# Two heads' attention scores in one product, with decay and mask as a tile from GpSimd

## The chip, the core and the metric

The kernel runs on one core of a Trainium2 chip. A core has a tensor engine (TensorE, PE in the profile), a vector engine (VectorE, DVE), a scalar engine (ScalarE, ACT), GpSimd (POOL), and a sync engine (SyncE, SP), which here only issues DMAs. They run side by side, each through its own queue in order, and wait for each other by semaphores. SBUF is the on-chip memory; products land in PSUM, from which VectorE and ScalarE read. The metric is the device time of one execution in microseconds.

## The reference

One streaming step of a small encoder: 256 new frames of one stream (the prompt) and 64 new frames of another, which has 256 past frames in a cache (the sample). There are two layers; each is a SwiGLU channel mixer, a token mixer and a second channel mixer. The first layer's token mixer is a gated convolution, the second's is the forgetting attention, which the change touches:

```python
def fox_attend(q, k, v, c_q, c_k, q_pos, k_pos):
    s = jnp.einsum('bqhd,bkhd->bhqk', q, k) * (HEAD_DIM ** -0.5)
    decay = c_q[..., :, None] - c_k[..., None, :]        # per head; sums of log forget gates
    mask = k_pos[None, :] <= q_pos[:, None]
    s = jnp.where(mask, s + decay, NEG_INF)
    p = jax.nn.softmax(s, axis=-1)
    return jnp.einsum('bhqk,bkhd->bqhd', p, v)
```

There are 16 heads of 64 channels. The prompt's 256 queries see the prompt's keys at or before them; the sample's 64 queries see the 256 cached keys and the sample's own keys at or before them.

## The kernel before

All 320 frames (256 of the prompt, 64 of the sample) go through the dense products together, features on the partitions and frames along the free axis. Each weight comes from memory in slabs of 1024 x 256 (`wr`), is split by ScalarE into a rounded part (`wh`, line 121) and by VectorE into the rest (`wl`, line 122), and each dense product is three products of 320 columns (lines 141 to 143). Three slabs fit in each pool, so a new slab is loaded and split when an old one has been multiplied.

The attention layer works on pairs of heads, eight in all; a pair fills 128 partitions. The projections give q, k and v of a pair (`pq`, `pk`, `pv`), and four generators follow them:

- `gates` makes the log forget gates and their running sums, negated and scaled for the keys (`nck`) and scaled for the queries (`cq`), one row per head.
- `decay_rows` loads these rows into the operands of the score product.
- `qk_heads` turns q and k frame-major (`qt`), normalises them (`sq` on GpSimd, then VectorE), turns them back (`np`), and writes them, with the cached keys (`kps`), to `qa` and `ka`. For each head these have its 64 channels in one half of the partitions; in the other half are zeros but for two rows, one of ones and one with the decay. So one product over 128 rows gives scores plus decay.
- `attend` makes the scores. The sample queries of both heads come first, as two products of 64 columns of queries each (`ss`, line 625), then each head's prompt queries in two blocks of 128 over 128 and 256 keys (`sc`, line 632), the second head's some dense products later. Each block goes through `softmax`: line 612 adds the mask and takes the row's extreme, line 614 exponentiates and sums, lines 615 and 616 divide. Then the probabilities are transposed (`tps`, `tpp`), copied by ScalarE (`pst`, `ppt`) and multiplied by the values into `oT` (lines 663 to 671). The sample's own values lie on 64 rows of the third tile of `vtok`.

Four PSUM banks (`aux`) serve all of these small products; a fifth request waits until the oldest bank is read out.

The order on TensorE is written out by a small planner at the end of `attn_mixer`. It walks through the dense products at 0.41 a group of three and puts in each step of a generator as soon as its delay (`LAT`, and the numbers that the generators yield) is over. The other engines' order is made by a scheduler from the program's order and the buffers. GpSimd's and SP's queues hold what they issue in that order, whatever is ready.

Of the kernel before, what the change touches and what calls it, by code (L numbers as in the profile page):

```python
# [16 lines left out]
P = 128  # L17
D = 1024
KD = D // P
S = 256  # L20
# [25 lines left out]
def trunk_kernel(  # L46
# [21 lines left out]

    def aux(name):
# [75 lines left out]
    # ---------------------------------------------------------------- constants and inputs  # L145
# [11 lines left out]
    # the first products' operands come in pieces of a few contraction tiles  # L157
# [26 lines left out]
    # ---------------------------------------------------------------- residual stream and norms  # L184
# [51 lines left out]
    # ---------------------------------------------------------------- x in  # L236
# [62 lines left out]
    # ---------------------------------------------------------------- attention: constants and small inputs  # L299
# [5 lines left out]
    for g, src in ((gq, q_norm), (gk, k_norm)):  # L305
        for hh in range(2):
# [4 lines left out]
    mask1 = const.tile([P, 2 * P], F32, tag="mask1", name="mask1")  # L311
    nc.gpsimd.memset(mask1, 0.0)
    nc.gpsimd.affine_select(out=mask1[:, P:], in_=mask1[:, P:], compare_op=ALU.is_ge, fill=NEG,
                            base=0, pattern=[[-1, P]], channel_multiplier=1)
    masks = const.tile([P, PAST + TS], F32, tag="masks", name="masks")
    nc.gpsimd.memset(masks, 0.0)
    for hh in range(2):
        m = masks[hh * TS:(hh + 1) * TS, 0:TS]
        nc.gpsimd.affine_select(out=m, in_=m, compare_op=ALU.is_ge, fill=NEG, base=0,
                                pattern=[[-1, TS]], channel_multiplier=1)  # L320

    # Per pair of heads: rows of one head's channels, and in the other half two rows that add
    # the decay c_q - c_k to the scores.
    qa, ka = [], []
    for b in range(2):
        q = const.tile([P, 2, T], F32, tag=f"qa{b}", name=f"qa{b}")
        k = const.tile([P, 2, NK], F32, tag=f"ka{b}", name=f"ka{b}")
        for t in (q, k):
            nc.gpsimd.memset(t[0:HD, 1], 0.0)
            nc.gpsimd.memset(t[HD:P, 0], 0.0)  # L330
            nc.gpsimd.memset(t[HD:HD + 2, 0], 1.0)
            nc.gpsimd.memset(t[0:2, 1], 1.0)
        qa.append(q)
        ka.append(k)
    # ones where a frame counts into the sum of a later one
# [10 lines left out]
    # ---------------------------------------------------------------- channel mixer  # L346
# [76 lines left out]
    # ---------------------------------------------------------------- gated convolution  # L423
# [54 lines left out]
    # ---------------------------------------------------------------- forgetting attention  # L478
    def attn_mixer(next_gain, pool):
# [3 lines left out]
        cq = pool.tile([H, T], F32, tag="cq", name="cq")  # L483
        r2T = pool.tile([P, 3], F32, tag="r2T", name="r2T")
        st = {"decay": False, "rows": set(), "scored": [0] * KD, "v": set(), "done": [0] * KD}

        def gates(pf):
            fr = pool.tile([H, T], F32, tag="fr", name="fr")
# [7 lines left out]
            # forget gates, frame-major  # L496
# [13 lines left out]
            # log1p(e) = 2 artanh(e / (2 + e))  # L510
# [14 lines left out]
            # sums of the log gates up to each frame, head-major: prompt; past and sample  # L525
# [10 lines left out]
            TSC(cq[:, 0:S], cp[:H, 0:S], 8.0, None, ALU.mult)  # L536
            TSC(cq[:, S:T], cs[:H, PAST:PAST + TS], 8.0, None, ALU.mult)
            st["decay"] = True
            yield 1.8, 0.0

        def decay_rows(p):
            while not (st["decay"] and (p < 2 or st["scored"][p - 2] == 2)):
                yield 0.0, 0.0
            b = p % 2
            for hh in range(2):
                h = 2 * p + hh
                row = HD if hh == 0 else 0
                nc.sync.dma_start(out=ka[b][row:row + 1, hh], in_=nck[h:h + 1])
                nc.sync.dma_start(out=qa[b][row + 1:row + 2, hh], in_=cq[h:h + 1])
            yield 0.0, 4.0  # L550
            st["rows"].add(p)

        def qk_heads(p, pq, pk, kpast, vpast, vtok):
# [5 lines left out]
            # normalised per head, frame-major; the gains are left for later  # L559
# [22 lines left out]
            ktok = pool.tile([P, 3, P], F32, tag="ktok", name="ktok", bufs=2)  # L582
# [12 lines left out]
            nc.scalar.copy(out=ka[b][0:HD, 0, T:NK], in_=kps[0:HD, 0:PAST])  # L595
            nc.vector.tensor_copy(ka[b][HD:P, 1, T:NK], kps[HD:P, 0:PAST])
            for n, g, dst in zip(qkn, (gq, gk), (qa[b], ka[b])):
# [3 lines left out]
                nc.scalar.activation(dst[0:HD, 0, 0:T], np_[0:HD, :T], AF.Copy, scale=g[0:HD])  # L601
                TSC(dst[HD:P, 1, 0:T], np_[HD:P, :T], g[HD:P], None, ALU.mult)
# [228 lines left out]
```

## Time and profile before

| what | value |
|---|---|
| median of the runs | 1251.88 us (1251.42 to 1253.5, 3 runs) |
| the profiled execution, first to last instruction | 1250.0 us |
| TensorE, VectorE, ScalarE, GpSimd busy | 1238.3, 763.0, 499.4, 52.2 us |
| attention stage (from the first q projection to the last output projection) | 832 to 1009 us |

The profiled execution shows one time, its span; the runs' median is 1.9 us above it. In the timeline a row is a start, a duration, the engine, the line, the operation, what it writes and reads, and the shape; `x4` is four records in a row, and a float32 product is two records, a transpose or one of the rounded dense products one. Durations of products overlap, so that the distance between starts tells what a product takes from the stream. A bracket at a row's end is the engine's idle time before it and what ended it. A row of waits has the total, the number and the longest. A row of a tile has the least, median and greatest duration in ns. A row of stretches has length, busy time of PE, PEld, DVE, ACT and POOL, granted clock, DMA share and GB/s.

### The profile page before, as it was taken

Reading aid. Unit: us, or ns where it says so; the run is one execution under the profiler, and the core shown is the slowest. Engines: PE = TensorE matmul, PEld = TensorE weight load, DVE = VectorE, ACT = ScalarE, POOL = GpSimd, SP = SyncE. Lnnn points to the kernel's source line nnn. Section 1 sums busy time; section 2 is a strip of 40 time slices with the busy share of each in tenths; the row PEclk is TensorE's granted clock in tenths of the full one; section 3 lists DMA queues with packets and bytes.
Section 4 is the critical chain, followed back from the end, with each engine's and each line's share of the span. In section 5 each row is a group of like instructions: output and inputs, shape, how many; then the busy total and the mean of one; then the engine's idle time right before and its main releaser. Section 6 shows DMA issues by size and latency. Waiting matters only on the chain.

```text
span 1250.0 us, 20886 instructions
## 1 busy us (share of the span) xinstructions
PE 1238.3 (99%) x8520; PEld 1216.8 (97%) x8520; DVE 763.0 (61%) x1403; ACT 499.4 (40%) x797; POOL 52.2 (4%) x102
## 2 busy tenths in 40 slices
PE   9999999999999999999999999999999999999998
PEld 7999999999999999999999999998898899999998
DVE  5756645576685656554665564558887676666432
ACT  6434333333433434333343433334656544343321
POOL 5000000000000000000000000002222000000000
PEclk9999999999999999999999999999999999999999
DMA  8544444444445444344444444454333154443440
GB/s 258 192 159 145 148 140 152 155 150 146 158 136 161 143 153 151 126 155 159 153 151 144 160 128 151 126 172 120 111 126 122 51 192 146 146 158 129 162 136 22
DMA packets 186128, 180.93 MB, mean 145 GB/s; under 512 B 8644, under 2 KB 185952, under 8 KB 186032
## 3 DMA queue, kind: packets, MB, share of 16 engines
q1 hardware_dynamic: 184880, 178.95, 44.4%
q8 instruction: 67, 1.10, 0.4%
q10 hardware_dynamic: 768, 0.54, 0.2%
q0 software_dynamic: 384, 0.11, 0.2%
q14 instruction: 29, 0.24, 0.1%
HBM read 175.54 MB, written 3.97 MB: 144 GB/s over the span
## 4 chain that ended last, share of the span: by engine, by line
PE 93%; DVE 4%; issue 1%; DMA 1%; ACT 1%; POOL 1%; POOLq 0%; ACTq 0%; SPq 0%; DVEq 0%
PE po L142 8%; PE po L143 8%; PE po L141 8%; PE pa L141 8%; PE pa L142 8%; PE pb L143 8%; PE pb L142 8%; PE pa L143 8%; PE pb L141 8%; PE pc L142 2%; PE pc L141 2%; PE pc L143 2%; PE pm L142 2%; PE pm L143 2%; PE pm L141 1%; DVE wl L122 1%
## 5 line engine op out<-in xcount | busy, mean ns | idle before, releaser
L122 DVE TENSOR_TENSOR wl<-wr,wh 128x1024 fp32r<-128x1024 f32 (+2 forms) x340 | 399.2, 1196 | 174.9 <-ACT wh L121 171.1
L121 ACT CAST wh<-wr 128x1024 fp32r<-128x1024 f32 (+2 forms) x337 | 333.5, 1018 | 423.6 <-issue 190.4
L141 PE MATMUL po<-gh,wh 128*128 128x320 f32 x704 | 217.0, 308 | 0.0
L142 PE MATMUL po<-gl,wh 128*128 128x320 f32 x704 | 216.5, 308 | 0.0
L143 PE MATMUL po<-gh,wl 128*128 128x320 f32 x704 | 216.5, 308 | 0.0
L141 PE MATMUL pa<-xh,wh 128*128 128x320 f32 x688 | 213.0, 310 | 0.0
L143 PE MATMUL pa<-xh,wl 128*128 128x320 f32 x688 | 213.0, 310 | 0.0
L142 PE MATMUL pa<-xl,wh 128*128 128x320 f32 x688 | 212.9, 310 | 0.0
L141 PE MATMUL pb<-xh,wh 128*128 128x320 f32 x688 | 212.8, 309 | 0.0
L142 PE MATMUL pb<-xl,wh 128*128 128x320 f32 x688 | 212.8, 309 | 0.0
L143 PE MATMUL pb<-xh,wl 128*128 128x320 f32 x688 | 212.8, 309 | 0.0
L142 PEld LDWEIGHTS po<-gl,wh 128*128 128x128 f32 x704 | 131.9, 187 | 0.0
L141 PEld LDWEIGHTS po<-gh,wh 128*128 128x128 f32 x704 | 131.9, 187 | 0.0
L143 PEld LDWEIGHTS po<-gh,wl 128*128 128x128 f32 x704 | 131.9, 187 | 0.0
L141 PEld LDWEIGHTS pa<-xh,wh 128*128 128x128 f32 x688 | 129.3, 188 | 0.1
L143 PEld LDWEIGHTS pa<-xh,wl 128*128 128x128 f32 x688 | 129.3, 188 | 0.0
L142 PEld LDWEIGHTS pa<-xl,wh 128*128 128x128 f32 x688 | 129.3, 188 | 0.0
L141 PEld LDWEIGHTS pb<-xh,wh 128*128 128x128 f32 x688 | 129.2, 188 | 0.0
L142 PEld LDWEIGHTS pb<-xl,wh 128*128 128x128 f32 x688 | 129.2, 188 | 0.0
L143 PEld LDWEIGHTS pb<-xh,wl 128*128 128x128 f32 x688 | 129.2, 188 | 0.0
L364 DVE TENSOR_TENSOR at<-pa,R_f 128x320 f32<-128x320 f32 x86 | 41.9, 488 | 113.2 <-PE pa L143 113.0
L378 DVE TENSOR_TENSOR bt<-pb,R_f 128x320 f32<-128x320 f32 x86 | 42.3, 492 | 63.5 <-PE pb L143 63.3
(269 smaller groups left out, 1560.5 us busy)
## 6 DMA issues: line engine op xcount, KB each, us to landing
wr<-in_ffn_w_in_dram SPq DMA_DIRECT2D x172, 512.0 KB
wr<-in_ffn_w_out_dram SPq DMA_DIRECT2D x64, 512.0 KB
wr<-in_ffn_w_out_dram SPq DMA_DIRECT2D x32, 384.0 KB
wr<-in_conv_w_in_dram SPq DMA_DIRECT2D x24, 512.0 KB
wr<-in_attn_w_in_dram SPq DMA_DIRECT2D x24, 512.0 KB
wr<-in_conv_w_out_dram SPq DMA_DIRECT2D x8, 512.0 KB
wr<-in_attn_w_out_dram SPq DMA_DIRECT2D x8, 512.0 KB
wr<-in_ffn_w_in_dram SPq DMA_DIRECT2D x4, 384.0 KB
```

Of the source, the lines that this page charges most:

```text
L121: nc.scalar.copy(out=h[:, ks], in_=r[:, ks])
L122: TT(out=l[:, ks], in0=r[:, ks], in1=h[:, ks].bitcast(F32), op=ALU.subtract)
L141: nc.tensor.matmul(ps, lhsT=wh, rhs=xh, start=first, stop=False)
L142: nc.tensor.matmul(ps, lhsT=wh, rhs=xl, start=False, stop=False)
L143: nc.tensor.matmul(ps, lhsT=wl, rhs=xh, start=False, stop=last)
L364: TT(out=at, in0=pa[:, :T], in1=R, op=ALU.mult)
L378: TT(out=bt, in0=pb[:, :T], in1=R, op=ALU.mult)
```

## The change

The score product no longer carries the decay. The queries of a pair are held in five tiles of 64 frames (four of the prompt, one of the sample), block-diagonal: a tile has 128 columns, 64 of each head, with the other head's half of the partitions zero. The keys of both heads lie below each other in one `ka` without zeros. One product per tile then gives the scores of both heads, 128 rows, over 64, 128, 192 and 256 prompt keys, or over the 320 keys of the sample.

Decay and mask come as a tile from GpSimd. `nck` is written to a scratch tensor in DRAM and read back with each head's row repeated over 64 partitions; `cq` is transposed by TensorE to one column per tile (`ct`, `cqT`). For each tile of queries GpSimd adds the column to the row, and a triangle of 64 columns (`causal`) to the diagonal part. The softmax reduction takes this tile in place of the mask.

The probabilities of a pair lie in one `pt` with blocks of zeros where a 128-wide transpose reaches over the diagonal. The sample's values are transposed as a full third tile, the last 64 prompt frames in its other rows; the matching probabilities are zero.

```diff
-LAT = dict(rstd=2.5, raw=1, norm=12, evac=4.5, soft=4.5, pt=1, vr=2, next=1.5)
+LAT = dict(rstd=2.5, raw=1, norm=12, evac=4.5, soft=6.5, pt=1, vr=2)
+QT = 5
+SCW = (TS, 2 * TS, 3 * TS, 4 * TS, PAST + TS)
+SCO = (0, TS, 3 * TS, 0, 0)
+PRO = (0, P, 2 * P, 4 * P, 6 * P + TS)
...
-            TSC(cq[:, 0:S], cp[:H, 0:S], 8.0, None, ALU.mult)
-            TSC(cq[:, S:T], cs[:H, PAST:PAST + TS], 8.0, None, ALU.mult)
+            cq = pool.tile([H, QT, 2, TS], F32, tag="qk", name="cq", bufs=2)
+            for i, c in enumerate((cp[:H, 0:S], cs[:H, PAST:PAST + TS])):
+                c = c.rearrange("p (i q) -> p i q", q=TS)
+                n = c.shape[1]
+                TSC(cq[:, 4 * i:4 * i + n], c[:, :, None, :].to_broadcast([H, n, 2, TS]), 8.0, None, ALU.mult)
+            nc.sync.dma_start(out=nckd, in_=nck)
+            yield 1.8, 1.5
+            ct = aux("ct")
+            for i in range(QT):
+                nc.tensor.transpose(ct[:, i * H:(i + 1) * H],
+                                    cq[:, i].rearrange("p h q -> p (h q)"), ident[:H, :H])
...
-        def decay_rows(p):
+        def decay_tile(p):
             while not (st["decay"] and (p < 2 or st["scored"][p - 2] == 2)):
                 yield 0.0, 0.0
...
+            d = pool.tile([P, 6 * TS + NK], F32, tag="dec", name=f"dec{p}", bufs=2)
+            rows = d[:, 6 * TS:]
             for hh in range(2):
                 h = 2 * p + hh
-                row = HD if hh == 0 else 0
-                nc.sync.dma_start(out=ka[b][row:row + 1, hh], in_=nck[h:h + 1])
-                nc.sync.dma_start(out=qa[b][row + 1:row + 2, hh], in_=cq[h:h + 1])
-            yield 0.0, 4.0
-            st["rows"].add(p)
+                nc.sync.dma_start(out=rows[hh * TS:(hh + 1) * TS], in_=nckd[h:h + 1].to_broadcast([TS, NK]))
...
+            for i, n in enumerate(SCW):
+                keys = slice(0, n) if i < QT - 1 else slice(S, NK)
+                src = dst = rows[:, keys]
+                if i < QT - 2:
+                    dst = d[:, o:o + n]
+                    o += n
+                nc.gpsimd.tensor_scalar(dst, src, cqT[:, p, i:i + 1], None, ALU.add)
+                diag = dst[:, n - TS:n] if i < QT - 1 else dst[:, 0:TS]
+                nc.gpsimd.tensor_tensor(out=diag, in0=diag, in1=causal, op=ALU.add)
+                dts.append(dst)
+            yield 0.0, 8.0
+            st["rows"][p] = dts
...
-            nc.scalar.copy(out=ka[b][0:HD, 0, T:NK], in_=kps[0:HD, 0:PAST])
-            nc.vector.tensor_copy(ka[b][HD:P, 1, T:NK], kps[HD:P, 0:PAST])
+            nc.vector.tensor_copy(ka[b][:, T:NK], kps[:, 0:PAST])
...
+            for i, n in enumerate(SCW):
+                bank = max(0, i - 2)
+                if bank not in banks:
+                    banks[bank] = aux(f"sc{bank}")
+                keys = ka[b][:, 0:n] if i < QT - 1 else ka[b][:, S:NK]
+                nc.tensor.matmul(banks[bank][:, SCO[i]:SCO[i] + n], lhsT=qa[b][:, i].rearrange("p h q -> p (h q)"),
+                                 rhs=keys, start=True, stop=True)
+            for i, n in enumerate(SCW):
+                softmax(banks[max(0, i - 2)][:, SCO[i]:SCO[i] + n], dts[i], pt[:, PRO[i]:PRO[i] + n], f"{i}_{p}")
             st["scored"][p] = 2
-            yield 0.65, LAT["soft"]
+            yield 1.65, LAT["soft"]
...
+            for name, cols, heads_first in (("k0", (0, P, 2 * P, 4 * P), True), ("k1", (3 * P, 5 * P), True),
+                                            ("ks", (6 * P, 7 * P, 8 * P), False)):
...
-                    if c == 0:
-                        nc.tensor.matmul(oT[r, S:T], lhsT=vtok[:TS, 2, hc], rhs=pst[:TS, 0, q], start=True, stop=False)
-                    else:
-                        nc.tensor.matmul(oT[r, S:T], lhsT=vpast[:, c - 1, hc], rhs=pst[:, c, q], start=False, stop=(c == 2))
+                    q = slice(c * P + hh * TS, c * P + (hh + 1) * TS)
+                    nc.tensor.matmul(oT[r, S:T], lhsT=vtok[:, 2, hc] if c == 0 else vpast[:, c - 1, hc], rhs=kt[2][:, q],
+                                     start=(c == 0), stop=(c == 2))
```

The order of the instructions moves with it. On TensorE, at the third pair (pair 2), the program before had the sample scores, the first head's two blocks, the values' transposes, and then dense products; the second head's two blocks come nine products later:

```order
L625 MATMUL ss<-ka_371,qa_370 64x320 x2
L632 MATMUL sc<-ka_371,qa_370 128x128
L632 MATMUL sc<-ka_371,qa_370 128x256
L684 MATMUL vps<-ident,vr 128x128 x2
L684 MATMUL vps<-ident,vr 64x128
L141 MATMUL pq<-xh,wh_8860 128x320
```

In the change the five products of the pair stand together, three dense products further on (after 15 of the pq products in place of 12), and the cached keys' transposes of the next pair (`kps`, `np`) follow nine products behind `vps`:

```order
L663 MATMUL sc_9057<-ka_370,qa_367 128x64
L663 MATMUL sc_9057<-ka_370,qa_367 128x128
L663 MATMUL sc_9057<-ka_370,qa_367 128x192
L663 MATMUL sc_9061<-ka_370,qa_367 128x256
L663 MATMUL sc_9063<-ka_370,qa_367 128x320
L712 MATMUL vps<-ident,vr 128x128 x3
L149 MATMUL pq<-xh,wh_8876 128x320
```

So one block of scores, in three PSUM banks (`sc` with three numbers), has taken the place of two.

On SP, where the first pairs' decay is loaded, the program before had eight small loads among the weights (`wr`) and the keys' output (`ktok`):

```order
L115 DMA wr_8859<-in_attn_w_in_dram 128x4x256
L548 DMA ka_371<-nck 1x16x36
L549 DMA qa_370<-cq 1x16x20
L548 DMA ka_371<-nck 1x16x36
L587 DMA out_dram<-ktok 128x2x128
L588 DMA out_dram<-ktok 64x128
L549 DMA qa_370<-cq 1x16x20
```

Now it has the write to DRAM and, behind the first pair's keys, the four broadcast reads:

```order
L123 DMA wr_8875<-in_attn_w_in_dram 128x4x256
L549 DMA nckd<-nck 16x576
L123 DMA wr_8875<-in_attn_w_in_dram 128x4x256
L620 DMA out_dram<-ktok 128x2x128
L621 DMA out_dram<-ktok 64x128
L570 DMA dec_8388<-nckd 64x576 x2
L570 DMA dec_8401<-nckd 64x576 x2
L123 DMA wr_8884<-in_attn_w_in_dram 128x4x256 x2
```

The first read has moved behind the keys' output of its pair, and the second half of the weight slab ahead of it.

On GpSimd the squares of q and k (`sq`) and the keys with their gain (`ktok`) had the queue to themselves; at the third pair it now holds, ahead of that pair's squares, its tile:

```order
L579 TENSOR_SCALAR dec_8617<-dec_8617,cqT 128x64
L579 TENSOR_SCALAR dec_8617<-dec_8617,cqT 128x128
L581 TENSOR_TENSOR dec_8617<-dec_8617,causal 128x64
L579 TENSOR_SCALAR dec_8617<-dec_8617,cqT 128x192
L581 TENSOR_TENSOR dec_8617<-dec_8617,causal 128x64
L579 TENSOR_SCALAR dec_8617<-dec_8617,cqT 128x320
L581 TENSOR_TENSOR dec_8617<-dec_8617,causal 128x64
L579 TENSOR_SCALAR dec_8617<-dec_8617,cqT 128x256
L581 TENSOR_TENSOR dec_8617<-dec_8617,causal 128x64 x2
L604 TENSOR_TENSOR sq_8787<-n_8785 128x384
L604 TENSOR_TENSOR sq_8796<-n_8794 128x384
```

These ten operations per pair are new; the squares stand behind them in the same queue.

More of the change, by code (lines that the diff above doesn't have):

```diff
@@ L310, in trunk_kernel @@
     nc.gpsimd.dma_start(out=gkf, in_=k_norm.to_broadcast([P, HD]))
[L311 to L316, printed above, removed]
+    causal = const.tile([P, TS], F32, tag="causal", name="causal")
+    nc.gpsimd.memset(causal, 0.0)
     for hh in range(2):
-        m = masks[hh * TS:(hh + 1) * TS, 0:TS]
+        m = causal[hh * TS:(hh + 1) * TS]
         nc.gpsimd.affine_select(out=m, in_=m, compare_op=ALU.is_ge, fill=NEG, base=0,
@@ L637, in attend @@
-            st["scored"][p] = 2
-            yield 0.65, LAT["soft"]
-            pst = pool.tile([P, 3, P], F32, tag="pst", name=f"pst{p}", bufs=1)
-            tp = aux("tps")
-            nc.tensor.transpose(tp[:TS, 0:P], ps[:, 0:TS], ident)
-            for c in range(2):
-                nc.tensor.transpose(tp[:, (c + 1) * P:(c + 2) * P], ps[:, TS + c * P:TS + (c + 1) * P], ident)
-            nc.scalar.copy(out=pst[:TS, 0], in_=tp[:TS, 0:P])
-            nc.scalar.copy(out=pst[:, 1:3], in_=tp[:, P:3 * P].rearrange("p (c q) -> p c q", q=P))
@@ L647, in attend @@
-            ppt = []
-            for hh in range(2):
-                tp = aux("tpp")
-                nc.tensor.transpose(tp[:, 0:P], pr[2 * hh][:, 0:P], ident)
-                nc.tensor.transpose(tp[:, P:2 * P], pr[2 * hh + 1][:, 0:P], ident)
-                nc.tensor.transpose(tp[:, 2 * P:3 * P], pr[2 * hh + 1][:, P:2 * P], ident)
-                pp_ = pool.tile([P, 3, P], F32, tag=f"ppt{hh}", name=f"ppt{p}{hh}", bufs=1)
-                nc.scalar.copy(out=pp_, in_=tp[:, 0:3 * P].rearrange("p (c q) -> p c q", q=P))
-                ppt.append(pp_)
+            pt, dts = pts[b], st["rows"][p]
@@ L682, in values @@
             vps = aux("vps")
[L683 to L686 removed]
+            for c, t0 in enumerate(TOKF):
+                nc.tensor.transpose(vps[:, c * P:(c + 1) * P], vr[:, t0:t0 + P], ident)
+            nc.scalar.copy(out=vtok[:, :, fs], in_=vps[:, 0:3 * P].rearrange("p (c f) -> p c f", f=P))
             if p % 2 == 1:
@@ L713, in dense @@
             for p in range(KD):
[L714 removed]
+                side.append([decay_tile(p), 0.0])
             wq, wk = next_slab(), next_slab()
```

100 lines of the change are left out of this document (52 added, 48 removed).

## The prediction

> **What bounds the kernel now.** I read the page first, its busy times and then its chain of waits.
>
> ```profile
> PE 1238.3 (99%) x8520; PEld 1216.8 (97%) x8520; DVE 763.0 (61%) x1403; ACT 499.4 (40%) x797; POOL 52.2 (4%) x102
> PE 93%; DVE 4%; issue 1%; DMA 1%; ACT 1%; POOL 1%; POOLq 0%; ACTq 0%; SPq 0%; DVEq 0%
> ```
>
> TensorE works in 99% of the span and is 93% of the chain. Nothing else can be the limit of the whole, so an edit is worth what it takes from TensorE's own stream, plus or minus the waits that it makes there. The table by stretches gives the stage that is edited:
>
> ```profile
> 832.00:1009.00 177.00, 172.77 (x1296) 157.84 (x1294) 141.09 (x455) 95.79 (x235) 29.81 (x26) 1.00 0.37 114
> ```
>
> That is 177 us, with TensorE at the full clock (1.00), VectorE busy 141 us, ScalarE 96 and GpSimd 30. VectorE has 36 us to spare here, which matters below. A busy matmul is not a matmul at its peak (they overlap), so I price PE work by the starts in its timeline. First a place with the products of one head's prompt scores alone:
>
> ```profile
> 880.07 0.31 PE L143 MATMUL pq<-xh,wl 128*128 128x320 f32 x1
> 880.22 0.82 PE L632 MATMUL sc<-ka,qa 128*128 128x128 f32 x4
> 880.68 0.50 PE L141 MATMUL pq<-xh,wh 128*128 128x320 f32 x1
> 881.02 0.31 PE L142 MATMUL pq<-xl,wh 128*128 128x320 f32 x1
> 881.17 0.31 PE L143 MATMUL pq<-xh,wl 128*128 128x320 f32 x1
> ```
>
> Dense products follow each other every 0.147 us. From 880.07 to 881.02 pass 0.95 us, two such steps and 0.66 us for the scores: 128 and 256 keys, two records each (a float32 product is two records), 768 columns of records at 0.86 ns.
>
> **What the change takes from TensorE.** *Scores.* The sample queries' two products sit ahead of one such pair:
>
> ```profile
> 967.80 0.30 PE L143 MATMUL pv<-xh,wl 128*128 128x320 f32 x1
> 968.04 0.76 PE L625 MATMUL ss<-ka,qa 128*64 128x320 f32 x4
> 968.73 0.92 PE L632 MATMUL sc<-ka,qa 128*128 128x128 f32 x4
> ...
> 969.63 0.31 PE L142 MATMUL pv<-xl,wh 128*128 128x320 f32 x1
> ```
>
> 1.83 less 0.29 is 1.54 us, so the sample products cost 0.88 beyond the 0.66 of the others. They fill half the columns each (128*64) and run side by side, but the stream pauses going in (968.04 where 967.95 was due) and coming out. A pair of heads pays 1.54 + 0.66 = 2.20 us. Afterwards it is five full-width products over 64, 128, 192, 256 and 320 keys: 960 columns, 1920 of records, at 0.86 ns 1.65 us. The 64-key product is not in the trace. If its columns set its time it needs 0.11 us, if a full weight load does, two records at the 0.11 us at which the transposes below step, 0.22. I take the second, as the transposes are its nearest rows: 1.76 us. If the load's whole 0.19 us showed twice it were 1.92. Gain per pair 0.44 us (0.28 to 0.55), for eight pairs **3.5 us** (2.2 to 4.4).
>
> The Trainium skill, page "TensorEngine Tiling (Array Packing)", speaks for both sides of this row: "Key Properties" says that a switch of tiling mode drains the array, "Performance Considerations" that products with at most 64 stationary columns gain up to two-fold by column tiling. By the second alone the sample scores would cost 2 x 0.27 = 0.55 us and the gain would shrink by 2.7 us; the 0.88 of the trace agrees with the first.
>
> *Values.* The sample part of the output product starts with its own frames on half the rows (64*64):
>
> ```profile
> 877.62 0.88 PE L663 MATMUL oT<-ppt,vtok 128*64 128x128 f32 x12
> 878.42 0.33 PE L669 MATMUL oT<-pst,vtok 64*64 64x64 f32 x4
> 878.68 0.45 PE L671 MATMUL oT<-pst,vpast 128*64 128x64 f32 x8
> 879.07 0.87 PE L567 MATMUL qt<-ident,qk 128*128 128x128 f32 x6
> ```
>
> Those four records hold the place for 0.26 us and the eight after them, of the same width and length, for 0.39 us with the way out; the stream also stands before each change of shape. The twelve records ahead go in couples that step 0.11 us, so the next couple is due at 878.33; from there to 879.07 are 0.74 us, about 0.1 of it the way out. With 128 rows throughout (the values' last tile is now a full one, and the probabilities are zero against its foreign rows) all twelve sample records have one shape: six couples at half the columns and so half the step, 0.35, and the same way out. Gain 0.30 us a pair, **2.4 us** in all. If the pauses came from the operands and not from the shape it is 0; the same gap stands in every pair, so I keep 2.4.
>
> *Transposes* are nine a pair before and after (the six of L567 above take 0.65 us, 0.11 each), the 128 rows of zeros add none.
>
> **What it adds.** *The queries' decay as a column.* Five new transposes of cq stand twelve products after the sums, where now a projection goes on:
>
> ```profile
> 851.67 0.31 PE L141 MATMUL pv<-xh,wh 128*128 128x320 f32 x1
> 851.65 0.41 DVE L536 TENSOR_SCALAR cq<-cp 16x256 f32<-16x256 f32 x1
> 852.06 0.20 DVE L537 TENSOR_SCALAR cq<-cs 16x64 f32<-16x64 f32 x1
> ```
>
> TensorE is there at 851.67. VectorE ends cq at 852.26 today; both writes double (512 and 128 columns; 0.20 more per 192, so +0.27 and +0.07), to 852.6. That is a wait of 1.0 us and five steps of about 0.1: **+1.5**, of which 0.2 comes back, since the next transposes' wait for qk (below) falls into it.
>
> *Waits.* What TensorE waits for in this stage:
>
> ```profile
> PE vps L684 <- DVE vr L680: 0.9, 1, 0.9
> PE sc L632 <- DVE sts L612: 0.5, 1, 0.5
> PE np L600 <- DVE st L612: 0.4, 1, 0.4
> PE np L600 <- ACT vtok L686: 0.4, 1, 0.4
> PE vps L684 <- ACT qa L601: 0.3, 1, 0.3
> PE qt L567 <- ACT qk L557: 0.2, 1, 0.2
> ```
>
> The first goes: the scores now stand ahead of vps and cover it, **-0.9**. The four between are about PSUM buffers, 1.6 us. They change form. In an even pair the scores take three of the four small banks at once, then vps the fourth, and kps and two np need the three back, which the five reductions free. These stand behind the splitting of a weight slab:
>
> ```profile
> 897.64 0.31 PE L141 MATMUL pq<-xh,wh 128*128 128x320 f32 x1
> 899.94 2.86 DVE L122 TENSOR_TENSOR wl<-wr,wh 128x1024 fp32r<-128x1024 f32 x2
> 902.72 0.48 DVE L612 CUSTOM_DVE_ANT_0 ps<-ss,masks 128x320 f32<-128x320 f32 x1
> ```
>
> The reductions start 5.1 us after the pq product that frees the slab. In pair 2 the changed stream reaches kps after 15 products, 1.8 us of scores, vps (three transposes, 0.33) and 9 products: 5.6 us. With 0.48 us for 320 columns and less in proportion for fewer, the third reduction ends near 6.0, the fifth near 6.9, so about 1.0 us is lost; pairs 0 and 4 have 18 products there and lose perhaps half of that. 2.0 in place of 1.6: **+0.4** (0 to +4, the upper end with both slab halves lengthened as in the GpSimd rows below).
>
> *The last pair* has nothing dense to hide behind:
>
> ```profile
> 987.26 0.27 PE L642 MATMUL tps<-ident,ps 128*64 128x128 f32 x1
> 988.80 1.25 PE L663 MATMUL oT<-ppt,vtok 128*64 128x128 f32 x12 [0.39 <-ACT ppt L654]
> 990.23 0.45 PE L671 MATMUL oT<-pst,vpast 128*64 128x64 f32 x8
> ```
>
> Today both prompt copies come after the sample copies; from 987.26 to the end of oT are 3.4 us. Now the first copy holds key tile 0 of both heads, so eight of the twelve prompt records start after it, near +1.4, and the end is near +2.7: **-0.7**. The softmax itself has 30 products ahead of it (4.4 us) where it had 18.
>
> *GpSimd's tile.* Per pair two broadcast loads of 147 KB on SP, then five additions of a column over 960 columns and five of the triangle over 320. No addition of a column is in the trace. The nearest rows:
>
> ```profile
> L571 POOL TENSOR_TENSOR sq<-n x16: 821/826/1798, 844.9 to 962.8; 128x384 f32<-128x384 f32 x16
> L583 POOL TENSOR_TENSOR ktok<-n,gkf x8: 992/1470/3071, 853.7 to 970.1; 128x384 f32<-128x384 f32 x8
> L337 POOL MEMSET tri<- 128x320 f32 x1 | 0.4, 369 | 0.1
> L122 DVE TENSOR_TENSOR wl<-wr,wh 128x1024 fp32r<-128x1024 f32 x33 | 43.5, 1338 | 2.7 <-ACT wh L121 2.6
> L122 DVE TENSOR_TENSOR wl<-wr,wh x42: 1206/1218/2043, 825.4 to 1026.5; 128x1024 fp32r<-128x1024 f32 x42
> ```
>
> By the memset (about 1 ns a column) and an undisturbed sq (2.1) a tile is some 2.5 us, by the slowest sq (4.7) 6. It is hidden: pair 2's tile is released when pair 0's reductions end, some 3 us after the row below starts, and needed at 902.7. Only pair 0 is tight. nck is written just ahead of cq (851.65), goes to DRAM and back, and the read is queued on SP behind the keys' output. That waits for ktok, whose first start of 853.7 moves 1 us with the work behind ct, and which takes up to 2 us; with the issues between, the read leaves at about 858. What a landing takes is bounded by the last two rows:
>
> ```profile
> 867.74 0.48 DVE L612 CUSTOM_DVE_ANT_0 ps<-ss,masks 128x320 f32<-128x320 f32 x1
> out_dram<-lf POOLq DMA_DIRECT2D x1, 16.0 KB, 2.0
> gkf<-in_k_norm_dram POOLq DMA_DIRECT2D x1, 32.0 KB, 7.1
> ```
>
> so the tile is ready between 862 and 871, and VectorE wants it at 867.74. 0 to 4 us lost; SP's queue has no row of its own, I take **0**.
>
> VectorE loses one gain product a pair (0.56 us) and gains cq's columns; ScalarE copies in three pieces in place of four. Both have room.
>
> **Sum.** -3.5 - 2.4 + 1.5 - 0.2 - 0.9 + 0.4 - 0.7 = -5.8 us. The profiled span of 1250.0 becomes 1244.2. The runs' median, 1251.88, lies 1.9 above that span, and I carry the difference over: **1246.0 us**, 0.5% faster.
>
> **Rivals.**
> *The reductions become the gate.* If the slab halves take 2.0 us as the slowest wl does, each even pair loses 1 to 1.6 us more and the odd pairs' transposes meet unfinished softmax too: 4 to 5 us given back, 1250 to 1251. For it: one block of five softmaxes in place of two smaller ones. Against: 4.8 us of dense products (33 or more) pass between a pair's scores and its transposes. 14%.
>
> *GpSimd blocks VectorE* (the slower side). The place is the whole stage: wl takes 1.22 us as a rule and 2.04 at worst, and I put the difference down to ktok and sq, of which 1.8 and 3.1 us at worst stand beside 0.8 and 1.0 at best. New GpSimd work is 8 x 2.5 to 8 x 6, 20 to 48 us. If VectorE stands still for all of it, its 141 us less about 6 plus 48 are 183, over the 171 that TensorE then needs: the stage lasts 183, 6 us more than today, 1258. It decides from 36 us of blocking on. Against it: 30 us of GpSimd now cost wl 33 x 0.12 = 4 us. 11%. The Trainium skill, page "SBUF — State Buffer", section "SBUF: two separate sides", states this rule: the port pair of VectorE and GpSimd is an exclusive lock for operations with two SBUF inputs. The 2.04 beside 1.22 agrees.
>
> *The first tile is late* by the 4 us above, pair 1's behind it: 1250 to 1252. 5%.
>
> *The half-array products cost what their columns say* (0.55 us, two of 320 columns at 0.86 ns running side by side), the pauses stay elsewhere in the stream, and the change removes less than it says: 2.7 us less gain, 1248.7. That is the tiling page's rule above without its drain. Against it the 0.88 measured. 10%.
>
> **How the numbers follow.** The forecast has 60%. Its own span is 1243 to 1248.5; the low end takes both TensorE terms at their best. The first and third rivals lie near the old time, the second above. The range of 1242.5 to 1252.5 leaves the second out and little else. Faster by over 0.2% (2.5 us, about what a measurement of this kernel tells from none): forecast, the half-array case and a little of the others, 0.72. Within: 0.16. Slower: 0.12.
>
> **What would show it.** Right: scores as five full-width products in about 1.75 us with no pause around them; oT's sample records with no gap; TensorE busy in the stage near 166. Wrong: PE waiting for st or pt of the softmax more than 2.5 us in all, ct waiting over 1.5, VectorE's reductions waiting for POOL after pair 0, wl's mean far above 1338 ns, or the 64-key records stepping 0.19 us.

## The result and the profile after

| | before | changed |
|---|---|---|
| median of the runs | 1251.65 us (1251.41 to 1253.5, 4 runs) | 1266.07 us (1264.84 to 1266.51, 4 runs) |
| the profiled execution | 1250.0 us | 1263.1 us |
| GpSimd busy | 52.2 us | 93.1 us |

The changed kernel takes 1.0114 times as long (95% interval 1.0102 to 1.0126). The forecast was 1246.0 us with a range of 1242.5 to 1252.5: the sign was wrong, and the time lies 13.6 us above the range.

The page and the table by stretches of the changed kernel:

```profile
PE 1240.2 (98%) x8509; PEld 1222.9 (97%) x8509; DVE 758.8 (60%) x1397; ACT 494.7 (39%) x773; POOL 93.1 (7%) x174
PE 89%; POOL 5%; DVE 3%; DMA 1%; issue 1%; ACT 1%; SPq 0%; POOLq 0%; DVEq 0%; ACTq 0%
832.00:1022.00 190.00, 174.62 (x1281) 163.62 (x1280) 136.66 (x448) 90.34 (x210) 77.68 (x106) 0.96 0.38 118
```

GpSimd, 1% of the chain before, is 5% of it now. The stage ends near 1022 instead of 1009, all of the loss lies in it, and its mean granted clock is 0.96 instead of 1.00. So two things are new: TensorE waits, and it runs slower for a time.

What TensorE waits for in the stage (the three longest entries), and what VectorE waits for, first before, then changed:

```profile
PE np L632 <- DVE n L613: 3.7, 1, 3.7
PE vps L712 <- DVE vr L708: 3.6, 1, 3.6
PE vps L712 <- DVE t L216: 2.7, 1, 2.7
```

```profile
DVE m L572 <- POOL sq L571: 6.1, 14, 1.7
```

```profile
DVE m L605 <- POOL sq L604: 21.9, 14, 7.2
```

TensorE's new waits are for VectorE, and VectorE's are for `sq`, the squares that GpSimd makes for the normalisation: 21.9 us instead of 6.1. No one waits for the tile itself: VectorE's waits in the stage have no entry for it. Followed back from the first of TensorE's long waits (rows of SP, GpSimd, ScalarE, VectorE and TensorE, picked from the timeline of the changed kernel):

```profile
871.18 0.96 POOL L579 TENSOR_SCALAR dec<-dec,cqT 128x256 f32<-128x256 f32 x1
872.39 1.00 POOL L616 TENSOR_TENSOR ktok<-n,gkf 128x384 f32<-128x384 f32 x1
873.42 0.38 SPq L620 DMA_DIRECT2D out_dram<-ktok  x1
875.62 1.10 SPq L570 DMA_DIRECT2D dec<-nckd  x2
879.91 0.86 ACT L602 COPY n<-qt 128x384 f32<-128x384 f32 x2
882.03 1.02 POOL L579 TENSOR_SCALAR dec<-dec,cqT 128x64 f32<-128x64 f32 x2 [8.36 <-DMA dec<-nckd]
886.60 0.60 POOL L581 TENSOR_TENSOR dec<-dec,causal 128x64 f32<-128x64 f32 x2
887.16 1.61 POOL L604 TENSOR_TENSOR sq<-n 128x384 f32<-128x384 f32 x2
888.02 0.55 DVE L605 TENSOR_REDUCE m<-sq 128x6 f32<-128x384 f32 x1 [7.23 <-POOL sq L604]
895.92 1.03 DVE L613 TENSOR_TENSOR n<-n,y 128x384 f32<-128x384 f32 x2
896.63 1.51 PE L632 MATMUL np<-ident,n 128*128 128x128 f32 x6 [3.69 <-DVE n L613]
```

Read it downwards. Pair 1's tile holds up pair 1's `ktok` on GpSimd to 872.39. SP's queue holds the store of `ktok` and behind it the row loads of pair 2, so these are issued at 875.62, where the last reduction to read their buffer had ended at 870.06. They have landed by 882.03, 6.4 us after the issue. Meanwhile pair 2's `n` is ready for its squares (the first from about 880.3), but GpSimd's queue has the tile ahead: it starts at 882.03, ends at 887.2, and only then come the squares. VectorE, in order too, stands 7.23 us, with the splitting of the next weight slabs behind it, and TensorE stands 3.69 us for `n`.

The wait of 2.7 us near the end has another shape. Pair 7's rows are issued at 964.35, as soon as their buffer is free, and its tile starts at 968.21. Beside a working VectorE it takes, with one `ktok` among its instructions, until 977.4, and VectorE then stands 4.8 us for the squares behind it. So here it is the length of the tile that counts.

Then the clock. Dense products that stepped 0.147 us step 0.267 us behind the waits. The second of them, and a stretch behind it:

```profile
899.27 0.47 PE L151 MATMUL pv<-xh,wl 128*128 128x320 f32 x1
903.37 0.90 PE L712 MATMUL vps<-ident,vr 128*128 128x128 f32 x3 [3.63 <-DVE vr L708]
...
904.30:909.40 5.10, 5.10 (x20) 5.10 (x20) 3.98 (x12) 2.47 (x3) 1.02 (x1) 0.50 0.39 129
```

In the stretch of 904.3 to 909.4 TensorE is busy throughout, with 20 records (a run below has 39 in it), at a granted clock of 0.50. Steps of 0.267 us stand in three places, 32 in all: 32 x 0.12 = 3.8 us.

### The profile page after: what moved, and what is told of

It reads as the page before. It is cut to its first block, busy times and chain, and to the rows that moved or that the text cites. A ratio compares the mean times of both kernels' runs of the same rounds, so it can differ in the third digit from the quotient of the medians.

```text
span 1263.1 us, 20880 instructions
## 1 busy us (share of the span) xinstructions
PE 1240.2 (98%) x8509; PEld 1222.9 (97%) x8509; DVE 758.8 (60%) x1397; ACT 494.7 (39%) x773; POOL 93.1 (7%) x174
## 4 chain that ended last, share of the span: by engine, by line
PE 89%; POOL 5%; DVE 3%; DMA 1%; issue 1%; ACT 1%; SPq 0%; POOLq 0%; DVEq 0%; ACTq 0%
PE po L150 8%; PE po L151 8%; PE po L149 8%; PE pa L149 8%; PE pa L150 8%; PE pb L149 8%; PE pa L151 8%; PE pb L151 8%; PE pb L150 8%; POOL dec L579 2%; PE pc L150 2%; PE pc L151 2%; PE pc L149 2%; PE pm L150 2%; PE pm L149 1%; PE pm L151 1%
```

## The experiments

**The theory** is that a queue is blocked: the squares stand behind a tile, which may itself stand behind a load, VectorE waits in order, TensorE waits for VectorE and loses its clock besides. **Rivals**: *contention* (GpSimd's arithmetic slows VectorE's own instructions, as the prediction's second rival had it) and *late loads* (the rows come too late for the scores themselves).

**No arithmetic on the tile.** The five additions of a column and of the triangle are left out:

```diff
-                nc.gpsimd.tensor_scalar(dst, src, cqT[:, p, i:i + 1], None, ALU.add)
-                nc.gpsimd.tensor_tensor(out=diag, in0=diag, in1=causal, op=ALU.add)
```

> The changed kernel without GpSimd's arithmetic on the decay tile: the rows are loaded as they are and the reductions read them. It leaves out the queries' share of the decay and the causal mask. The loads and all waits for buffers stay. Queue theory and contention theory agree here that the kernel is fast, 1242 to 1247 us: this gives the price of the arithmetic as a whole. Late-load theory (the loads as such make the reductions late): the kernel stays above 1256 us, and VectorE's reductions wait for the row loads in pairs 2 to 7.

Measured: 1244.2 us (one run), span 1242.5. VectorE's wait for the squares and the stretch in which the changed kernel ran at half clock:

```profile
DVE m L599 <- POOL sq L598: 6.4, 14, 1.7
904.30:909.40 5.10, 5.10 (x39) 5.04 (x38) 0.27 (x4) 1.67 (x4) 0.00 (x0) 1.00 0.64 194
```

The arithmetic as a whole costs 22 us. Loads and waits for buffers alone cost nothing here, but they are not as late as in the changed kernel: with nothing ahead of `ktok`, pair 2's rows are issued at 868.70. What speaks against late loads as such is the changed kernel itself, in which no reduction waits for its tile. The rest of the change is then about as good as forecast, which is told below. Of the 20.6 us between the two spans, 3.8 are the slow steps; the view of TensorE's waits lists 14.8 us in the one and 2.1 in the other, 12.7 more. The last 4 us are in neither list (short waits, and small products at the slow clock).

**The squares on VectorE.** One line moves `sq` out of GpSimd's queue:

```diff
-                nc.gpsimd.tensor_tensor(out=sq, in0=n, in1=n, op=ALU.mult)
+                TT(out=sq, in0=n, in1=n, op=ALU.mult)
```

> The changed kernel with one line altered: the squares of a pair's normalisation (sq) are made by VectorE instead of GpSimd. GpSimd keeps the whole decay tile. Queue theory: sq stood behind the tile in GpSimd's queue, and the tile behind a late load; with sq out of that queue the waits of 3.4 to 4.65 us of the values and of the normalised queries go, and with them the stretches in which dense products step 0.267 us instead of 0.147. Stage 832 to 1022 about 170 to 174 us, granted clock 1.00, the kernel 1243 to 1248 us. VectorE gets 16 squares of about 0.5 us more and may lose 1 or 2 us of that. Contention theory: GpSimd's arithmetic slows VectorE's own instructions beside it; nothing of that is taken away and VectorE has 8 us more to do, so the kernel stays at 1264 us or above, and the waits for VectorE stay.

Measured: 1251.25 us, 0.9994 of before (0.9984 to 1.0003). This is between the two theories: 15 of the 22 us are gone, 7 are left. The next run divides these.

> The two edits before this together: the squares on VectorE and no arithmetic on the tile. It leaves out the queries' share of the decay and the causal mask. Against the run with the squares on VectorE and the whole tile (1251.25 us) it tells what the tile's arithmetic costs where no square stands behind it. Contention theory: most of the 22 us lie there, so this run is near 1244 us, 7 us below. Queue theory: once the squares are out of GpSimd's queue, the tile's arithmetic is nearly free, and what is left above 1244 is the price of 16 squares on VectorE, so 1248 to 1251 us.

Measured: 1249.98 us (one run). The totals would leave 1.3 us for the whole tile with no square behind it, but this execution came to the stage late. The first q projection and the first product behind the stage (`pa`), with the tile's arithmetic, then without:

```profile
832.08 0.31 PE L149 MATMUL pq<-xh,wh 128*128 128x320 f32 x1
...
1007.99 0.31 PE L149 MATMUL pa<-xh,wh 128*128 128x320 f32 x1
```

```profile
834.84 0.31 PE L149 MATMUL pq<-xh,wh 128*128 128x320 f32 x1
...
1007.22 0.30 PE L149 MATMUL pa<-xh,wh 128*128 128x320 f32 x1
```

The 2.8 us arise ahead of everything that the edit touches, and what they come from is open. Between these rows the stage takes 175.9 us with the tile's arithmetic and 172.4 without; with neither the arithmetic nor squares on VectorE it takes 169.2 (832.23 to 1001.40). So the tile costs 3.5 us where no square stands behind it, and the squares on VectorE cost 3.2, by one execution each. By the total this run lies where the queue theory had it, by the stage between the two. Part of the latter is a new wait: VectorE comes later to the forget gates, and the sums on TensorE stand for them.

```profile
PE cp L535 <- DVE t L215: 2.2, 1, 2.2
854.90:856.60 1.70, 1.70 (x8) 1.70 (x8) 1.70 (x7) 0.00 (x0) 0.00 (x0) 0.50 1.07 361
```

That wait ends at 852.18, and the clock is down behind it here too. Contention exists, but it is the smaller share. In the view of the tile `y`, VectorE's instruction of 12 columns in these two runs, first with the tile's arithmetic, then without (least, median, greatest ns):

```profile
L213 DVE TENSOR_SCALAR y<-m x8: 167/232/468, 847.9 to 967.0; 128x12 int32<-128x12 int32 x8
```

```profile
L213 DVE TENSOR_SCALAR y<-m x8: 165/173/174, 850.6 to 965.9; 128x12 int32<-128x12 int32 x8
```

So it is stretched beside GpSimd's additions. TensorE's waits for the softmax's reductions (`kps` behind `st`) are 1.7 us in all with the arithmetic and 0.5 without. Over the stage all of this comes to no more than the 3.5 us.

**The same work on GpSimd, in two other orders.** The first puts a pair's tile behind that pair's squares; GpSimd keeps to the order of the program:

```diff
+            while p not in st["sq"]:
+                yield 0.0, 0.0
...
+            st["sq"].add(p)
...
-        with tc.manual_schedule(engines={nc.tensor.engine}):
+        with tc.manual_schedule(engines={nc.tensor.engine, nc.gpsimd.engine}):
```

> The changed kernel with the same instructions on the same engines, but GpSimd's order is that of the program, and a pair's tile arithmetic is issued after that pair's squares. Its loads are issued where they were. Queue theory: sq finds GpSimd free, the two long waits go, 1244 to 1249 us; what now stands behind the tile is ktok, whose output feeds a store and the next pair's row loads, so a late row load can still cost a microsecond or two. Contention theory: as much GpSimd work as before beside VectorE's reductions, so 1262 us or more. Late-load theory (the row loads are late for the scores themselves): the scores wait, by 3 us or more in pairs 2 and 7, and the kernel stays above 1256 us.

Measured: 1270.75 us, 1.0151 of before (1.0134 to 1.0168). By the number the contention theory held, by the trace it did not:

```profile
DVE m L607 <- POOL sq L606: 25.3, 15, 6.3
...
862.79 1.08 POOL L581 TENSOR_SCALAR dec<-dec,cqT 128x320 f32<-128x320 f32 x1
864.24 1.61 POOL L606 TENSOR_TENSOR sq<-n 128x384 f32<-128x384 f32 x2
```

The squares wait longer than ever. They are the next pair's: pair 0's tile, now after pair 0's `ktok`, stands ahead of pair 1's squares. The edit moved the block on by one pair, and the expectation had looked only at the pair itself. The second order was written with both neighbours in view:

```diff
+            if p % 2 == 1:
+                fire(p - 1)
...
+            if p % 2 == 1:
+                fire(p)
```

Here `fire(p)` issues the additions of pair p's tile. The first of these places is right behind the squares of an odd pair, the second right behind its `ktok`.

> The changed kernel with the same instructions on the same engines; only GpSimd's queue is ordered by hand, so that no pair's squares stand behind a tile: the tile of an even pair comes right after the squares of the odd pair that follows it, the tile of an odd pair right after that pair's ktok. The loads are issued where they were. Queue theory: the waits of 3.4 to 4.65 us and the slow stretches of TensorE go, 1244 to 1250 us; the odd pairs' ktok stand behind a tile now, and the weight loads behind their output on SP, which may cost one or two. If it were the amount of GpSimd work beside VectorE (or the arithmetic as such), it stays at 1262 us or above.

Measured: 1250.58 us, 0.9995 of before (0.9985 to 1.0005).

```profile
DVE m L613 <- POOL sq L612: 5.1, 15, 0.7
...
892.23 2.59 POOL L612 TENSOR_TENSOR sq<-n 128x384 f32<-128x384 f32 x2
894.80 0.44 POOL L584 TENSOR_SCALAR dec<-dec,cqT 128x64 f32<-128x64 f32 x1
...
901.13 1.00 POOL L626 TENSOR_TENSOR ktok<-n,gkf 128x384 f32<-128x384 f32 x1 [0.49 <-DVE n L623]
902.11 2.47 POOL L584 TENSOR_SCALAR dec<-dec,cqT 128x64 f32<-128x64 f32 x1
```

The same instructions on the same engines, and the order of one queue gives back 15.5 of the 22 us. The squares wait 5.1 us in all, less than before the change. Just above the range that was expected, it is still 6 us slower than without the arithmetic. Some 4 of the 6 us lie at one place, behind the first tile, where three waits for the softmax and for PSUM come close together (0.26, 0.51 and 1.46 us) and 11 slow steps follow:

```profile
867.44 0.44 PE L639 MATMUL kps<-ident,kpast 128*128 128x128 f32 x2 [0.26 <-DVE st L659]
868.38 0.55 PE L644 MATMUL np<-ident,n 128*128 128x128 f32 x3 [0.51 <-ACT vtok L726]
870.39 0.62 PE L644 MATMUL np<-ident,n 128*128 128x128 f32 x3 [1.46 <-DVE st L659]
```

TensorE waits for VectorE at two of these, and VectorE is busy without a pause there (3.3 of the 3.3 us from 867.0 on), beside GpSimd, so contention may have a part in the 6 us; that was not tested, and where the rest lies was not followed up.

**The row loads a pair earlier**, with a third buffer (and the sums `c_k` in two temporary tiles, written out by two stores):

```diff
-            while not (st["decay"] and (p < 2 or st["scored"][p - 2] == 2)):
+            while not (st["decay"] and (p < 3 or st["scored"][p - 3] == 2)):
```

> The changed kernel with a third buffer for the decay tile, so that the row loads and the tile of a pair may start when the pair three back has been scored instead of the one two back; the sums c_k lie in two temporary tiles instead of one and are written out by two stores. Queue theory: the tile of pair 2 is made some ten microseconds earlier, ahead of its squares' operands, so the squares mostly find GpSimd free: 1244 to 1252 us. Where a later tile is still put right ahead of a pair's squares, one stall of 2 to 4 us stays. Contention theory: the same work on GpSimd, only moved, so within 3 us of 1266.

Measured: 1263.93 us (one run), where the contention theory had it; the timeline of GpSimd shows why:

```profile
884.41 1.02 POOL L581 TENSOR_SCALAR dec<-dec,cqT 128x64 f32<-128x64 f32 x2 [5.41 <-DMA dec<-nckd]
...
889.52 0.82 POOL L606 TENSOR_TENSOR sq<-n 128x384 f32<-128x384 f32 x1
```

Pair 2's tile is indeed done early, by 879. But the scheduler now puts pair 3's tile ahead of pair 2's squares, and that tile waits for its own late load. TensorE stands 6.6 us for `n` there. An earlier load does not help while the order still lets a tile in front.

**One part alone: the values' full third tile**, put into the kernel before (`TOKF` for the values' transposes, the sample's probabilities behind 64 columns of zeros, one shape for all twelve records):

```diff
-                        nc.tensor.matmul(oT[r, S:T], lhsT=vtok[:TS, 2, hc], rhs=pst[:TS, 0, q], start=True, stop=False)
+                        nc.tensor.matmul(oT[r, S:T], lhsT=vtok[:, 2, hc], rhs=pst[:, 0, q], start=True, stop=False)
```

> The kernel before with one part of the change alone: the third tile of the values holds 128 frames instead of the 64 sample frames, and its probabilities stand behind 64 columns of zeros, so that the sample part of the output product has 128 rows throughout and one evacuation goes. Scores, masks and decay rows stay as before. By the prediction's term the gap inside the output product goes, 0.30 us for each of 8 pairs: 1249.0 to 1249.8 us against 1251.65. The rival of that term (the gap belongs to the row groups, not to the row count): no difference, 1251.2 to 1252.

Measured: 1249.52 us beside 1251.31, ratio 0.9989 (0.998 to 0.9998), a gain of 1.8 us (0.3 to 2.5). The term is confirmed, if narrowly, and its size (2.4) lies within the interval. The edit also saves ScalarE two copies a pair, which this run does not separate.

**Less work for the same result.** `c_q` is one number for all keys of a query, so the softmax drops it; only `c_k` and the mask are needed. The five pieces of a tile are laid out in DRAM (`nckd`, 960 columns), and GpSimd adds the triangle alone, in three instructions:

```diff
-                nc.gpsimd.tensor_scalar(dst, src, cqT[:, p, i:i + 1], None, ALU.add)
-                diag = dst[:, n - TS:n] if i < QT - 1 else dst[:, 0:TS]
-                nc.gpsimd.tensor_tensor(out=diag, in0=diag, in1=causal, op=ALU.add)
+            for o, step, n in ((0, P, 2), (DO[2] + P, TS, 1), (DO[3] + 3 * TS, TS, 2)):
+                diag = d[:, o:o + n * step].rearrange("p (a q) -> p a q", q=step)[:, :, 0:TS]
+                nc.gpsimd.tensor_tensor(out=diag, in0=diag, in1=causal[:, None, :].to_broadcast([P, n, TS]), op=ALU.add)
```

> The changed kernel with a tile that needs less of GpSimd: the queries' share c_q is the same for all keys of a query, so the softmax drops it, and it is left out; the five pieces of a tile come from DRAM ready made, in one row of 960 instead of 576 columns, and GpSimd adds the causal mask alone, three instructions of 64 or 128 columns in place. The transposes of c_q, their tile and their evacuation go (1.28 us of TensorE with a wait of 0.6). The squares stay on GpSimd and behind the tile. Queue theory: about 1.2 us of GpSimd a pair instead of 5.2 to 6.8, so the squares are late by the wait for the row loads alone: 1242 to 1247 us, faster than both kernels. Late-load theory: the tile still waits for its loads with the squares behind it, so a stall of 2 to 4 us stays in pair 2 and perhaps pair 7: 1247 to 1256 us. Contention theory: the tile's GpSimd work falls to about a fifth, and with it the loss: 1245 to 1249 us.

Measured: 1244.42 us, 0.9947 of before (0.9934 to 0.9959), faster than both kernels.

```profile
873.41 1.15 POOL L560 TENSOR_TENSOR dec<-dec,causal 128x128 f32<-128x128 f32 x3 [5.34 <-DMA dec<-nckd]
877.90 1.61 POOL L583 TENSOR_TENSOR sq<-n 128x384 f32<-128x384 f32 x2 [3.35 <-ACT n L581]
```

A tile takes 1.15 us where VectorE leaves GpSimd alone. With `ktok` of pair 1 no longer held up, pair 2's rows are there at 873.41, and its squares find GpSimd idle. The removed transposes of `c_q` brought nothing further against the run without arithmetic (1244.2).

**Waits of chosen size.** In this last version VectorE makes `vr` of pairs 2, 4 and 6 several times over:

```diff
-            TT(out=vr, in0=pv[:, :T], in1=st["R"], op=ALU.mult)
+            for _ in range({2: 5, 4: 8, 6: 12}.get(p, 1)):
+                TT(out=vr, in0=pv[:, :T], in1=st["R"], op=ALU.mult)
```

> The version that adds the mask alone (1244.42 us), with three waits of chosen size put into TensorE's queue: VectorE computes the values product vr of pair 2 five times over, that of pair 4 eight times and that of pair 6 twelve times, 0.486 us each, so that TensorE waits about 1.9, 3.4 and 5.3 us longer there; the result is the same. If a wait costs only its length, the kernel is 10 to 11 us longer, 1254 to 1256 us, with dense products stepping 0.147 us throughout. If a wait above 2 to 3 us also brings slower steps of 0.267 us, as behind the long waits of the changed kernel: none after the first wait, 3 to 5 us of loss in all after the two longer ones, 1257 to 1260 us.

Measured: 1266.66 us (one run), 22.2 us longer, more than either side expected (2.6 us of it lie ahead of the stage, unexplained, as in the run above that came late). The waits came out at 4.2, 4.4 and 6.2 us, since VectorE's other work is late behind the repeats too; so no short wait was tried here. The three, by what ended them, and the stretch behind the first:

```profile
PE vps L692 <- DVE vr L688: 10.5, 2, 6.2
PE vps L692 <- DVE y L219: 4.4, 1, 4.4
899.80:904.30 4.50, 4.50 (x18) 4.50 (x18) 1.53 (x4) 2.04 (x3) 1.01 (x1) 0.51 0.13 36
```

Behind each of the three the products step 0.267 us, 41 times in all: 4.9 us on top of the waits, in a kernel whose tile takes GpSimd little more than a microsecond. The slow clock follows from the wait, not from the tile's arithmetic.

## Why the prediction was wrong

**The step that failed** is the one on GpSimd's tile: "It is hidden: pair 2's tile is released when pair 0's reductions end, some 3 us after the row below starts, and needed at 902.7. Only pair 0 is tight", with 0 taken and 0 to 4 us as bounds. It is true of the tile, which nobody waits for. What was left out is what is queued behind it. The piece of the order shown ahead of the prediction has the squares standing behind a tile on GpSimd, and the prediction's own sum counted the waiting of the tile without the waiting behind it. A load that is late and harmless for its own reader held up a reader of another kind. Measured: 22 us, by the run without the arithmetic; 15.5 us of them by the order alone.

The same step had the tile too short. By undisturbed rows it was to take 2.5 us, by the slowest square 6. Pair 2's takes 882.03 to 887.2, 5.2 us, while VectorE stands idle, and pair 3's, beside a working VectorE, 888.75 to 895.7, 6.9 us. An instruction of 64 columns that lasts 0.44 us alone lasts up to 2.47 (894.80 and 902.11 in the hand-made order). For the landing of the rows 2.0 and 7.1 us were the bounds. From the issue to the start of the reader it was at most 6.4 in the changed kernel, but 8.0 in the run with the loads a pair earlier (876.39 to 884.41). And SP's queue, which had no row and was put at nothing, held pair 2's rows back from 870.06 to 875.62, behind the store of `ktok`.

**A thing not priced at all** is the clock: 3.8 us of slow steps. No stretch of the profile before shows it in this stage (1.00 throughout), so the prediction had no row for it, and no term that it could grow from.

**The terms for TensorE held.** The rows of the changed kernel, for the scores of a pair with nothing else around, then the output product of pair 0, `ct`, and the last pair:

```profile
995.01 0.31 PE L151 MATMUL pm<-ayh,wl 128*128 128x320 f32 x1
995.16 1.90 PE L663 MATMUL sc<-ka,qa 128*128 128x64 f32 x10
...
997.05 0.31 PE L150 MATMUL pm<-ayl,wh 128*128 128x320 f32 x1
```

```profile
877.73 0.88 PE L693 MATMUL oT<-k,vtok 128*64 128x128 f32 x12
...
878.88 0.87 PE L600 MATMUL qt<-ident,qk 128*128 128x128 f32 x6
```

```profile
851.20 0.31 PE L151 MATMUL pk<-xh,wl 128*128 128x320 f32 x1
852.14 0.45 PE L554 MATMUL ct<-ident,cq 16*128 16x16 f32 x5 [0.63 <-DVE t L216]
...
852.77 0.31 PE L150 MATMUL pv<-xl,wh 128*128 128x320 f32 x1
```

```profile
1001.30 0.82 PE L676 MATMUL tk<-ident,pt 128*128 128x128 f32 x6
...
1003.45 0.41 PE L698 MATMUL oT<-ks,vpast 128*64 128x64 f32 x8
```

- *Scores*: 997.05 - 995.01 less two steps is 1.75 us, expected 1.76.
- *Values*: 877.73 to 878.88 are 1.15 us where 877.62 to 879.07 were 1.45: 0.30, as expected.
- *ct*: 1.57 less two steps, 1.28 us with a wait of 0.63; 1.5 less 0.2 was expected.
- *Bank waits*: +0.4 was expected, on 1.6 of before. In the run without arithmetic the entries for `np`, `kps` and `sc` are gone and one of 0.2 us (`qt` behind `ka`) is new, so the five reductions in a row were no gate. 2.0 us in all were expected, and the term was off by nearly that, on the cautious side. The wait of `vps` for `vr`, 0.9, is down to 0.2.
- *Last pair*: 1001.30 to 1003.86 are 2.6 us, +2.7 was expected for 3.4.
- *The sum* was a span of 1244.2, 5.8 us less; the span of the run without arithmetic is 1242.5, and from the first q projection to the first `pa` it takes 169.2 us where the kernel before takes 175.9, 6.7 less. TensorE is busy there for 166.5 us, and near 166 was named as a sign of being right. (Two sums in the prediction are off by 0.1: 1251.88 less 5.8 is 1246.1, and 8 x 0.33 is 2.6.)

**The rivals.** *The reductions become the gate*, *the first tile is late* and *the half-array products cost what their columns say* did not come: the scores' gain is there in full. *GpSimd blocks VectorE* had the right side for the wrong reason: its sign was to be a longer `wl`, and from 832 to 1022 the mean of `wl` is 1312 ns, beside 1325 in the same stretch before. It had VectorE held up in the middle of its work by a shared resource; VectorE was held up by waiting for a result. The section on the two sides in the Trainium skill's page "SBUF — State Buffer", cited there, is not refuted: instructions beside each other do stretch, on both engines. But what a lock would cost was worked out from all of GpSimd's new work, and with the squares out of the way the price is 3.5 us.

Of the signs named as wrong ones, "VectorE's reductions waiting for POOL after pair 0" is the nearest, but it had the softmax's reductions in mind. The ones that waited were the normalisation's.

## What to carry to other kernels

New work on an engine that is 4% busy is free only if its queue is: for each instruction added, ask which one stands behind it, when that one's operands are ready, and who waits for it, and put work that itself waits for a load behind everything urgent of this pair and of the next. What is left then is the price of two engines working beside each other, 3.5 us here. Leave out, before moving it, what the softmax cancels. And where TensorE bounds the kernel, a wait of several microseconds costs more than its length.

## What the runs showed of the hardware

After a wait TensorE's granted clock falls to 0.50 and stays there for some 3 to 6 us. In the stage, waits of 2.7 us and up were followed by slow steps each time. So was the wait of 2.2 us for the forget gates with the squares on VectorE, and so were the three of 0.26, 0.51 and 1.46 us close together. So was one of 1.8 us in the run with the loads a pair earlier, but not at once: TensorE worked on at full clock until 974.7, 1.4 us after the wait, and then made 12 slow steps. Waits of 2.2 and 1.7 us in the run with the tile behind its own squares were not. So it isn't the length of a single wait that decides here. The Trainium skill's page "TensorE: Matmul & The Clock Gate", section "Part 1: The HAM clock gate (the "warmup" mystery)", has the clock at half rate after at least one idle window of about 3.4 us, and, with one core at work, only at full or half. The half rate agrees with the 0.50, the length does not with the waits of 2.2 and 1.8 us.

A read from DRAM that repeats a row over 64 partitions (144 KB) took up to 6.4 us from its issue on SP to the start of its reader in the changed kernel, and 8.0 us once in the run with the loads a pair earlier.
